# Strassen's seven half-block products for the gate and up projections of a three-block model

## The chip, the cores and the metric

The kernel runs on one core of one Trainium2 chip. The metric is device time in microseconds (us) of one execution; a time of a kernel is the median of its runs. The core has five engines with queues of their own: TensorE (PE; its weight loads are listed as PEld), VectorE (DVE), ScalarE (ACT), GpSimd (POOL) and SyncE (SP, which here issues DMAs). Each works through its queue in order and waits on semaphores for the others.

## The reference

A hidden state x of 512 tokens and 1024 features goes through three blocks: attention with compressed, selected and windowed keys; two layers of sparse and differential attention; and a state-space branch beside a delta rule. Each of the four layers ends in a gated feed-forward of inner width 2816, all in float32:

```
h = rms_norm(x, g)
gate, up = h @ w_gate, h @ w_up            # 1024 -> 2816 each
x = x + (silu(gate) * up) @ w_down         # layers 2, 3 and 4
# layer 1: up passes a causal convolution of width 3 first, then
# a, g = split(up);  x = x + (silu(g) * a) @ w_down
```

## The kernel before

Features lie on the 128 partitions and the 512 tokens along the free dimension, so x is eight tiles of 128x512. Every float32 operand of a large product is split in two float32r parts, hi and lo, and a product of a 128x128 weight tile with a 128x512 tile of x is three matmuls (`mm3`, L347 to L352): hi·hi, hi·lo, lo·hi. `load_piece` (L277) fetches a block of weights of 128x1024 by DMA (`wraw`, a ring of 4), ACT casts it to `whi` (L283) and DVE subtracts to get `wlo` (L284); `whi` and `wlo` have rings of 3 (WS). `lin_T` (L295) runs eight k-tiles of three matmuls into one PSUM bank.

A feed-forward (`ffn`, L1617) handles its 22 pairs of a gate block and an up block (128 inner features each) in two halves of 11, each followed by the down projection of that half (`out_proj`, L1628). For three of the four layers a pair is `swiglu` (L1606): product for the gate, DVE multiply by the row of 1/rms (`rbc`, L1610), Silu on ACT (L1611), a second multiply by `rbc` on POOL (L1612), product for up, DVE multiply with it (L1614), and the split of the result into `acth` and `actl` (L291, L292). In the first layer (`ff`, L843) each of the two products is multiplied by `rbc` (L848), convolved by an ACT operation (L851) and two DVE steps (L856), and gated (L858, L859).

`out_proj` of the mixer, ahead of the feed-forward, adds to x (L1634), makes the operand hi and lo of x·g for the feed-forward (`norm_in`, L467 on ACT and L468 on DVE), and adds squares of x into a sum (`stat_add`, L434 on ACT, L436 on POOL).

The order of the instructions of each engine is set by the framework's scheduler when the program is built; no table of the kernel sets it. Tiles of a ring are given out in turn, and a writer waits until the last reader of its slot is done.

Of the kernel before, what the change touches and what calls it, by code (L numbers as in the profile page):

```python
# [197 lines left out]
# ---------------------------------------------------------------- device code  # L198
class Build:
# [141 lines left out]
    def scaled(self, o, scale, name):  # L341
        """o * scale in two parts."""
# [4 lines left out]
    def mm3(self, out, w, x, start=True, stop=True):  # L347
        """out (+)= w.T @ x, either operand in two parts."""
# [5 lines left out]
    def scores(self, q, k, qt, masks, mx, sm):  # L354
        """Per half: exp(max - (q.k + mask)) with its row sums; q carries the turned sign."""
# [19 lines left out]
    def turned(self, t, qt):  # L375
        """[queries, keys] -> the blocks of keys on partitions, [128, block, 128 queries]."""
# [10 lines left out]
    def rsqrt(self, y, v, pool=False):  # L387
        """y = v ** -0.5 on small [128, n] tiles; v is SBUF and positive."""
# [17 lines left out]
    def bcast_cols(self, col_of_tt, tag="at"):  # L406
        """[128 tokens, 128 (broadcast)] stationary per token tile -> PSUM [128, 512] rows."""
# [5 lines left out]
    def bcast_pairs(self, cols, tag="at"):  # L413
        """cols [128 tokens, 4, 2] -> PSUM [128 = (2, 64), 512]."""
# [4 lines left out]
    # sums of squares of the residual stream, and what follows from them  # L419
# [19 lines left out]
    def col_sums(self, *accs):  # L439
        """-> PSUM [128 tokens, 4]: sums over the partitions."""  # L440
# [9 lines left out]
    def stat_end(self, st):  # L450
        """-> [128 tokens, 4]: 1 / rms"""
# [21 lines left out]
    # ------------------------------------------------------------ block 1  # L473
    def block1(self, x, B, first, g_next, stats):
# [36 lines left out]
        # the overlapping windows of the compressed keys and values, position pairs on partitions  # L511
# [99 lines left out]
        # relative bias strips, sign turned: strip[p, h, c] = -bias[bucket(p + 384 - c)], masked where negative  # L611
# [30 lines left out]
        # the two halves of the spatial gating unit, in parts that go between others  # L642
# [28 lines left out]
        # q / k norms per head  # L671
# [16 lines left out]
        # compressed branch probabilities, transposed to [(r, n), q]  # L688
# [85 lines left out]
        # selected and windowed branches, head pair by head pair: scores ahead of transposes and values, with parts  # L774
        # of projections in between
# [59 lines left out]
        hg = self.out_proj(x, self.aps["b1_wout"][:, :, :512], mix, B["g_ffn"], [st])  # L835
# [3 lines left out]
        # convolved gated feed-forward, in two halves of its width  # L839
        wup = self.aps["b1_wup"]  # L840
        self.set_ring(cv=3)

        def ff(f):  # L843
            cv = []
            for h in range(2):
                ps = self.lin_T(wup[2 * f + h], hg)
                up = self.r512("cv")
                nc.vector.tensor_tensor(up, ps, rbc, op=ALU.mult)  # L848
# [31 lines left out]
    def block2(self, l, x, xg, st, G, g_next, stats):  # L880
# [38 lines left out]
        # index scores and the 128 largest per query  # L919
# [54 lines left out]
        # A unit is a pair of heads (two maps of one, or two that share a block of rows), a step a unit's tile of  # L974
        # queries: scores two steps ahead, then transposes, then values, with parts of projections in between.
# [44 lines left out]
        # sparse attention over the selected keys  # L1020
# [725 lines left out]
```

## Time and profile before

| | before |
|---|---|
| median of three runs | 3123.3 us (3119.72 to 3123.72) |
| span of the profiled execution | 3123.8 us (with nothing listed around it) |
| PE busy | 3052.9 us, 98% |
| DVE busy | 1785.8 us, 57% |
| ACT busy | 1231.4 us, 39% |
| POOL busy | 440.5 us, 14% |
| bytes moved by DMA | 299.95 MB, mean 96 GB/s |

Busy time is the time in which an engine has at least one instruction under way. A matmul's record is longer than the distance from its start to the next one's start, since matmuls overlap; the pace of PE is read from starts. An instruction's record on DVE or POOL begins when the engine takes it up and includes any time that it stands before it can move data.

### The profile page before, as it was taken

To read this page: it belongs to the slowest core of one execution; us is meant where nothing else is said; L and a number is where in the kernel's file an instruction comes from. 1 tells how busy PE (TensorE), PEld (TensorE's weight loads), DVE (VectorE), ACT (ScalarE), POOL (GpSimd) and SP (SyncE) were. 2 spreads that over 40 slices of the span, in tenths; PEclk is the share of its full clock that TensorE was granted. 3 is DMA by queue.
4 is the path that set the end of the run, shared out by engine and by line. 5 is a ranking of instruction groups with operands and counts; after the bars stand their busy time and mean duration, and the time that the engine had idled before them with its cause. 6 is when DMAs were issued, how large, how long until landed. Compare 5 with 4: busy or idle time off the path is not lost.

```text
span 3123.8 us, 40875 instructions
## 1 busy us (share of the span) xinstructions
PE 3052.9 (98%) x15416; PEld 2437.1 (78%) x15416; DVE 1785.8 (57%) x3400; ACT 1231.4 (39%) x2261; POOL 440.5 (14%) x411
## 2 busy tenths in 40 slices
PE   8999999999999999999999999999999999999998
PEld 6867888887677888887677888877777888888886
DVE  6576655647976333348866333369874665543333
ACT  4365433434455222234454222347543433322222
POOL 0001000011221101121211101110820000211011
PEclk9999999998999999998899999999999999999999
DMA  5402223332212223332213233236434222322322
GB/s 175 125 22 77 90 80 109 99 100 81 74 52 92 95 81 108 97 99 80 72 47 99 93 91 102 79 107 199 155 99 155 85 86 88 108 95 78 110 83 74
DMA packets 124052, 299.95 MB, mean 96 GB/s; under 512 B 28440, under 2 KB 40792, under 8 KB 123856
## 3 DMA queue, kind: packets, MB, share of 16 engines
q1 hardware_dynamic: 115696, 285.79, 29.2%
q10 hardware_dynamic: 7680, 9.97, 1.2%
q8 instruction: 122, 2.00, 0.3%
q0 software_dynamic: 480, 1.57, 0.1%
q14 instruction: 74, 0.61, 0.1%
HBM read 272.52 MB, written 14.79 MB: 92 GB/s over the span
## 4 chain that ended last, share of the span: by engine, by line
PE 87%; DVE 6%; DMA 2%; ACT 2%; POOL 1%; issue 1%; ACTq 1%; SPq 0%; DVEq 0%; POOLq 0%
PE p L350 24%; PE p L351 24%; PE p L352 24%; PE s L362 2%; DMA rope<-rope 2%; PE tr L382 1%; PE ss L444 1%; PE p L333 1%; ACTq L874 1%; DVE isc L925 1%; PE O L1036 1%; PE p L335 1%; PE p L334 1%; POOL rope L877 1%; DVE m L924 1%
## 5 line engine op out<-in xcount | busy, mean ns | idle before, releaser
L350 PE MATMUL p<-xh,whi 128*128 128x512 f32 x2360 | 955.4, 405 | 10.6 <-ACT xh L467 7.2
L283 ACT CAST whi<-wraw 128x1024 fp32r<-128x1024 f32 (+4 forms) x528 | 495.5, 940 | 1181.3 <-PE p L351 851.5
L351 PE MATMUL p<-xl,whi 128*128 128x512 f32 x2360 | 949.4, 402 | 0.5 <-DVE xl L468 0.5
L352 PE MATMUL p<-xh,wlo 128*128 128x512 f32 x2360 | 946.5, 401 | 1.1 <-DMA wraw<-in_b_cw1k 1.1
L284 DVE TENSOR_TENSOR wlo<-wraw,whi 128x1024 fp32r<-128x1024 f32 (+4 forms) x528 | 599.9, 1138 | 325.1 <-ACT whi L283 311.9
L350 PEld LDWEIGHTS p<-xh,whi 128*128 128x128 f32 x2360 | 448.4, 190 | 120.9 <-issue 8.8
L352 PEld LDWEIGHTS p<-xh,wlo 128*128 128x128 f32 x2360 | 447.5, 190 | 107.5 <-issue 4.8
L351 PEld LDWEIGHTS p<-xl,whi 128*128 128x128 f32 x2360 | 448.2, 190 | 103.1 <-issue 5.0
L350 PE MATMUL p<-acth,whi 128*128 128x512 f32 x704 | 277.8, 395 | 0.0
L352 PE MATMUL p<-acth,wlo 128*128 128x512 f32 x704 | 277.7, 394 | 0.0
L351 PE MATMUL p<-actl,whi 128*128 128x512 f32 x704 | 277.5, 394 | 0.0
L1612 POOL TENSOR_TENSOR g<-g,rbc 128x512 f32<-128x512 f32 x66 | 114.0, 1728 | 808.5 <-ACT g L1611 808.5
L436 POOL TENSOR_TENSOR sqacc<-sqacc,sq 128x512 f32<-128x512 f32 x63 | 97.4, 1550 | 777.0 <-ACT sq L434 776.8
L1614 DVE TENSOR_TENSOR g<-g,p 128x512 f32<-128x512 f32 x66 | 45.4, 688 | 238.7 <-PE p L352 238.7
L352 PEld LDWEIGHTS p<-acth,wlo 128*128 128x128 f32 x704 | 132.2, 188 | 31.6
L351 PEld LDWEIGHTS p<-actl,whi 128*128 128x128 f32 x704 | 132.2, 188 | 31.5
L350 PEld LDWEIGHTS p<-acth,whi 128*128 128x128 f32 x704 | 132.2, 188 | 31.3
L1610 DVE TENSOR_TENSOR g<-p,rbc 128x512 f32<-128x512 f32 x66 | 45.7, 692 | 188.1 <-PE p L352 188.1
L369 ACT ACTIVATE stile<-stile,sm 128x128 f32<-128x128 f32 (+3 forms) x192 | 106.8, 557 | 83.3 <-DVE sm L366 72.1
L1634 DVE TENSOR_TENSOR x<-x,p 128x512 f32<-128x512 f32 x96 | 66.0, 688 | 108.1 <-PE p L352 107.9
L333 PE MATMUL p<-whi,xh 128*128 128x256 f32 (+2 forms) x352 | 104.6, 298 | 0.3 <-ACT rope L871 0.3
L334 PE MATMUL p<-wlo,xh 128*128 128x256 f32 (+2 forms) x352 | 102.9, 293 | 0.0
(457 smaller groups left out, 4183.4 us busy)
## 6 DMA issues: line engine op xcount, KB each, us to landing
wraw<-in_b_wup SPq DMA_DIRECT2D x176, 512.0 KB, 3.3
wraw<-in_b_win SPq DMA_DIRECT2D x118, 512.0 KB, 3.6
wraw<-in_b_wdn SPq DMA_DIRECT2D x64, 512.0 KB, 3.5
wraw<-in_b_wout SPq DMA_DIRECT2D x48, 256.0 KB, 2.7
wraw<-in_b_wdn SPq DMA_DIRECT2D x64, 192.0 KB, 2.3
rope<-rope ACTq DMA_DIRECT2D x128, 64.0 KB, 2.3
row<-rows SPq DMA_DIRECT2D x32, 256.0 KB, 4.4
wraw<-in_b_wtC SPq DMA_DIRECT2D x8, 512.0 KB, 4.0
```

Of the source, the lines that this page charges most:

```text
L283: nc.scalar.copy(hi, raw)
L284: nc.vector.tensor_tensor(lo, raw, hi.bitcast(F32), op=ALU.subtract)
L333: mm(ps, xs[k][0][:, ts], wh[:, s], start=k == 0, stop=False)
L334: mm(ps, xs[k][0][:, ts], wl[:, s], start=False, stop=False)
L350: mm(out, w[0], x[0], start=start, stop=False)
L351: mm(out, w[0], x[1], start=False, stop=False)
L352: mm(out, w[1], x[0], start=False, stop=stop)
L362: self.nc.tensor.matmul(out[g][:, :n], q[i][hs, qt * P : n], k[j][hs, :n], start=c == 0, stop=c == 2)
L369: nc.scalar.activation(t[:, :n], t[:, :n], AF.Exp, bias=mx[:, g : g + 1], scale=-1.0, accum_out=sm[:, g : g + 1])
L436: eng.tensor_tensor(accs[i], accs[i], sq, op=ALU.add)
L1612: nc.gpsimd.tensor_tensor(g, g, rbc, op=ALU.mult)
L1634: nc.vector.tensor_tensor(x[m], x[m], ps, op=ALU.add)
```

## The change

The products of a pair, the weight blocks A (gate above up, 256 inner features) by h (1024 features by 512 tokens), are taken as a 2x2 block product: A is halved by output (gate, up) and by features (k-tiles 0 to 3, 4 to 7), h by features and by tokens (0 to 255, 256 to 511). Strassen's algorithm, in Winograd's form, makes it from seven products of half blocks in place of eight: 84 matmuls of 256 columns for a pair in place of 48 of 512. The seven need sums of blocks on both sides.

- On the side of h, `Forms` makes them once per feed-forward, in the `out_proj` of the mixer, in place of `norm_in`.
- On the side of the weights, `load_pair` makes four sums of 128x512 per pair on POOL, and splits seven blocks of 128x512 in hi and lo (one split of 1024 columns and five of 512).
- `pair_steps` runs the products (PSUM banks 0 to 5) and combines them: two copies on ACT, five adds with a PSUM input on DVE, two adds on POOL, each of 256 columns. The up half comes out with its sign turned, and the last multiply turns it back.

New rings of four slots each: `ws` (sums of weights), `wa` (the seventh block in two parts), `gu` (gate and up).

```diff
+    def load_pair(self, wa, wb):
+        ...
+        a11, a12, a21, a22 = (r[:, o : o + T] for r in raws for o in (0, T))
+        s1, s2, s4, s3 = (self.r512("ws") for _ in range(4))
+        for o, i, j in ((s1, a21, a22), (s2, s1, a11), (s4, s2, a12), (s3, a11, a21)):
+            nc.gpsimd.tensor_tensor(o, i, j, op=ALU.add)
+        ...
+        both = self.split(raws[0], tiles=parts())
+        f = {"a11": [t[:, :T] for t in both], "a12": [t[:, T:] for t in both]}
+        for names, srcs in ((("s1", "s2"), (s1, s2)), (("s4", "s3"), (s4, s3)), (("a22",), (a22,))):
+            tiles = parts() if len(names) == 2 else [self.r512("wa", F32R) for _ in range(2)]
+            for i, (name, src) in enumerate(zip(names, srcs)):
+                f[name] = self.split(src, tiles=[t[:, i * T : (i + 1) * T] for t in tiles])
+        return f
+
+    def pair_steps(self, wa, wb, xf, g, u):
+        ...
+        def product(w, x):
+            ps = self.pst("st", "st")[:, :H]
+            for k in range(KT // 2):
+                c = slice(k * P, (k + 1) * P)
+                self.mm3(ps, [t[:, c] for t in f[w]], xf.parts[x][k], k == 0, k == KT // 2 - 1)
+            return ps
+
+        add = nc.vector.tensor_tensor
+        nc.scalar.copy(g[:, lo], product("a11", "b11"))
+        nc.scalar.copy(u[:, hi], product("s1", "t5"))
+        add(u[:, lo], g[:, lo], product("s2", "t6"), op=ALU.add)
+        add(g[:, lo], g[:, lo], product("a12", "b21"), op=ALU.add)
+        add(g[:, hi], u[:, hi], product("s4", "b22"), op=ALU.add)
+        nc.gpsimd.tensor_tensor(g[:, hi], g[:, hi], u[:, lo], op=ALU.add)
+        add(u[:, lo], u[:, lo], product("s3", "t7"), op=ALU.add)
+        nc.gpsimd.tensor_tensor(u[:, hi], u[:, hi], u[:, lo], op=ALU.add)
+        add(u[:, lo], u[:, lo], product("a22", "t4"), op=ALU.add)
...
     def swiglu(self, w, f, hg, rbc):
-        pg = self.lin_T(w[2 * f], hg)
-        g = self.tmp(name="g")
-        nc.vector.tensor_tensor(g, pg, rbc, op=ALU.mult)
+        g, u = self.r512("gu"), self.r512("gu")
+        last_of(self.pair_steps(w[2 * f], w[2 * f + 1], hg, g, u))
+        nc.vector.tensor_tensor(g, g, rbc, op=ALU.mult)
         nc.scalar.activation(g, g, AF.Silu)
         nc.gpsimd.tensor_tensor(g, g, rbc, op=ALU.mult)
-        pu = self.lin_T(w[2 * f + 1], hg)
-        nc.vector.tensor_tensor(g, g, pu, op=ALU.mult)
+        nc.vector.scalar_tensor_tensor(g, g, -1.0, u, op0=ALU.mult, op1=ALU.mult)
         return self.split(g, "act")
...
+class Forms:
+    def keep(self, src, *where):
+        both = self.b.split(src, "xf")
...
+    def add(self, m, x, g):
+        ...
+        if m < 4:
+            u = self.u[k] = b.t512(name="xu")
+            nc.scalar.activation(u, x, AF.Copy, scale=g)
+            nc.vector.tensor_tensor(u[:, hi], u[:, lo], u[:, hi], op=ALU.subtract)
+            self.keep(u, ("b11", k), ("t5", k))
+            return
+        ...
+        nc.scalar.activation(w, x, AF.Copy, scale=g)
+        nc.vector.scalar_tensor_tensor(t6, w[:, hi], -1.0, u[:, hi], op0=ALU.mult, op1=ALU.subtract)
+        self.keep(w, ("b21", k), ("b22", k))
+        nc.vector.scalar_tensor_tensor(v[:, hi], t6, -1.0, w[:, lo], op0=ALU.mult, op1=ALU.subtract)
+        nc.vector.scalar_tensor_tensor(v[:, lo], t6, -1.0, u[:, lo], op0=ALU.mult, op1=ALU.subtract)
+        if k % 2:
+            self.keep(self.t6, ("t6", k - 1), ("t6", k))
+        self.keep(v, ("t7", k), ("t4", k))
```

In the convolved feed-forward of the first layer the two products are replaced in the same way; the gate's half is then multiplied by `rbc` on POOL (L909 of the changed kernel) and the up half on DVE (L907).

Two places in the order show what stands in the queues. The first is DVE, in the middle of the first half of the first swiglu feed-forward, before the change: two pairs.

```order
L1610 TENSOR_TENSOR g_9849<-p_9824,rbc_9390 128x512
L284 TENSOR_TENSOR wlo_9927<-wraw_9924,whi_9926 128x1024
L1614 TENSOR_TENSOR g_9849<-g_9849,p_9859 128x512
L284 TENSOR_TENSOR wlo_9963<-wraw_9960,whi_9962 128x1024
L292 TENSOR_TENSOR actl_9886<-g_9849,acth_9885 128x512
L1610 TENSOR_TENSOR g_9920<-p_9895,rbc_9390 128x512
L284 TENSOR_TENSOR wlo_9998<-wraw_9995,whi_9997 128x1024
L1614 TENSOR_TENSOR g_9920<-g_9920,p_9930 128x512
L284 TENSOR_TENSOR wlo_10034<-wraw_10031,whi_10033 128x1024
L292 TENSOR_TENSOR actl_9957<-g_9920,acth_9956 128x512
```

At the same place after the change one pair (gu_11624, gu_11625) has fourteen rows, of which these are the first twelve (L1676, the product with the up half, and L292 for `actl` follow); `st` are the PSUM tiles of the products, `ws` the sums of weights, and the `wlo` rows make the parts of the next pair, the `wa` row those of the pair after it.

```order
L514 TENSOR_TENSOR gu_11625<-gu_11624,st_11686 128x256
L292 TENSOR_TENSOR wlo_11781<-wraw_11768,whi_11780 128x1024
L516 TENSOR_TENSOR gu_11624<-gu_11624,st_11700 128x256
L292 TENSOR_TENSOR wlo_11785<-ws_11772,whi_11784 128x512
L518 TENSOR_TENSOR gu_11624<-gu_11625,st_11714 128x256
L292 TENSOR_TENSOR wlo_11785<-ws_11773,whi_11784 128x512
L1673 TENSOR_TENSOR gu_11624<-gu_11624,rbc_11054 128x512
L521 TENSOR_TENSOR gu_11625<-gu_11625,st_11729 128x256
L292 TENSOR_TENSOR wlo_11791<-ws_11774,whi_11790 128x512
L292 TENSOR_TENSOR wlo_11791<-ws_11775,whi_11790 128x512
L524 TENSOR_TENSOR gu_11625<-gu_11625,st_11744 128x256
L292 TENSOR_TENSOR wa_11939<-wraw_11912,wa_11938 128x512
```

Five rows a pair have become fourteen, and the splits of weights, which stood one per product, stand between the adds of the pair in work.

The second place is POOL, at the same point of the program, before the change: five pairs.

```order
L1612 TENSOR_TENSOR g_9423<-g_9423,rbc_9390 128x512
L1612 TENSOR_TENSOR g_9494<-g_9494,rbc_9390 128x512
L1612 TENSOR_TENSOR g_9565<-g_9565,rbc_9390 128x512
L1612 TENSOR_TENSOR g_9636<-g_9636,rbc_9390 128x512
L1612 TENSOR_TENSOR g_9707<-g_9707,rbc_9390 128x512
```

After the change, one pair (gu_11624, gu_11625); the `ws` rows are the sums of weights of the pair after next.

```order
L482 TENSOR_TENSOR ws_11914<-wraw_11912 128x512
L519 TENSOR_TENSOR gu_11624<-gu_11624,gu_11625 128x256
L482 TENSOR_TENSOR ws_11915<-ws_11914,wraw_11910 128x512
L522 TENSOR_TENSOR gu_11625<-gu_11625 128x256
L482 TENSOR_TENSOR ws_11916<-ws_11915,wraw_11910 128x512
L1675 TENSOR_TENSOR gu_11624<-gu_11624,rbc_11054 128x512
L482 TENSOR_TENSOR ws_11917<-wraw_11910,wraw_11912 128x512
```

One row a pair has become seven, and the pair's own two sums and its multiply stand between the sums for a later pair.

## Rows read from the trace of the kernel before

**Rows 1.** The page's first part: busy us (share of span) xinstructions.
```profile
PE 3052.9 (98%) x15416; PEld 2437.1 (78%) x15416; DVE 1785.8 (57%) x3400; ACT 1231.4 (39%) x2261; POOL 440.5 (14%) x411
```
**Rows 2.** Windows, a swiglu half: us, then PE, PEld, DVE, ACT, POOL busy, PEclk.
```profile
1194.00:1305.00 111.00, 111.00 (x479) 89.73 (x478) 43.88 (x50) 31.24 (x40) 17.98 (x10) 1.00 0.28 89
```
**Rows 3.** Timeline of POOL, same half: start us, duration us, engine, line, operation.
```profile
1228.11 1.80 POOL L1612 TENSOR_TENSOR g<-g,rbc 128x512 f32<-128x512 f32 x1 [9.36 <-ACT g L1611]
1239.27 1.80 POOL L1612 TENSOR_TENSOR g<-g,rbc 128x512 f32<-128x512 f32 x1 [9.36 <-ACT g L1611]
```
**Rows 4.** Timeline of PE, same half: matmuls of 512 columns.
```profile
1232.02 0.39 PE L350 MATMUL p<-xh,whi 128*128 128x512 f32 x1
...
1232.71 0.39 PE L350 MATMUL p<-xh,whi 128*128 128x512 f32 x1
```
**Rows 5.** Timeline of PE, first layer's projections: matmuls of 256 columns.
```profile
135.78 0.41 PE L335 MATMUL p<-whi,xl 128*128 128x256 f32 x1
135.99 0.42 PE L333 MATMUL p<-whi,xh 128*128 128x256 f32 x1
...
136.37 0.28 PE L335 MATMUL p<-whi,xl 128*128 128x256 f32 x1
...
136.72 0.28 PE L335 MATMUL p<-whi,xl 128*128 128x256 f32 x1
```
**Rows 6.** Timeline of POOL in the last block, operations back to back.
```profile
2059.35 1.29 POOL L436 TENSOR_TENSOR sqacc<-sqacc,sq 128x512 f32<-128x512 f32 x1 [4.62 <-ACT sq L434]
2060.59 0.52 POOL L1288 MEMSET sys<- 128x512 f32 x1
...
2230.72 0.65 POOL L1298 TENSOR_TENSOR subst<-sys,sys 128x255 f32<-128x255 f32 x1
```
**Rows 7.** Timeline of DVE, a split of 1024 columns and its successor.
```profile
994.88 1.23 DVE L284 TENSOR_TENSOR wlo<-wraw,whi 128x1024 fp32r<-128x1024 f32 x1 [0.21 <-ACT whi L283]
996.02 0.75 DVE L468 SCALAR_TENSOR_TENSOR xl<-x,pack,xh 128x512 fp32r<-128x512 f32 x1
```
**Rows 8.** Timeline of DVE and POOL, the first layer's out projection.
```profile
292.34 1.34 POOL L436 TENSOR_TENSOR sqacc<-sqacc,sq 128x512 f32<-128x512 f32 x1 [140.26 <-ACT sq L434]
293.09 0.69 DVE L1634 TENSOR_TENSOR x<-x,p 128x512 f32<-128x512 f32 x1 [0.56 <-PE p L352]
293.69 0.69 DVE L284 TENSOR_TENSOR wlo<-wraw,whi 128x512 fp32r<-128x512 f32 x1
```
**Rows 9.** Lines by form: count | busy us, mean ns of one | idle before.
```profile
L292 DVE TENSOR_TENSOR actl<-g,acth 128x512 fp32r<-128x512 f32 x66 | 45.2, 685 | 0.0
...
L366 DVE CUSTOM_DVE_ANT_0 stile<-s,b_cmask 128x256 f32<-128x256 f32 x16 | 6.6, 414 | 0.9 <-PE s L362 0.9
...
L856 DVE SCALAR_TENSOR_TENSOR cv<-cv,pack,cv 128x511 f32<-128x511 f32 x44 | 32.8, 746 | 0.8 <-ACT cv L851 0.8
...
L291 ACT CAST acth<-g 128x512 fp32r<-128x512 f32 x66 | 41.0, 622 | 0.0
```
**Rows 10.** Timeline of DVE and POOL where both work, in the second block.
```profile
1489.02 0.69 DVE L876 TENSOR_TENSOR rope<-rope,tab 128x512 f32<-128x512 f32 x1
1489.15 1.70 POOL L875 TENSOR_TENSOR rope<-rope,tab 128x512 f32<-128x512 f32 x1 [7.42 <-DMA rope<-rope]
1489.63 2.30 DVE L284 TENSOR_TENSOR wlo<-wraw,whi 128x1024 fp32r<-128x1024 f32 x1
1490.93 2.12 POOL L877 TENSOR_TENSOR rope<-rope,rope 128x512 f32<-128x512 f32 x1
```
**Rows 11.** Windows, the out projection ahead of the second feed-forward.
```profile
984.50:1003.50 19.00, 18.26 (x83) 14.67 (x82) 15.43 (x19) 12.61 (x19) 7.99 (x6) 1.00 0.53 167
```
**Rows 12.** Windows, a stretch with pauses between matmuls (index scores).
```profile
741.00:748.30 7.30, 6.64 (x26) 4.54 (x28) 6.53 (x13) 3.78 (x8) 0.14 (x1) 0.50 0.00 0
```

More of the change, by code (lines that the diff above doesn't have):

```diff
@@ L834, in block1 @@
         st = self.stat()
-        hg = self.out_proj(x, self.aps["b1_wout"][:, :, :512], mix, B["g_ffn"], [st])
+        hg = Forms(self)
+        self.out_proj(x, self.aps["b1_wout"][:, :, :512], mix, B["g_ffn"], [st], forms=hg)
         self.free(mix)
@@ L840, in block1 @@
         wup = self.aps["b1_wup"]
-        self.set_ring(cv=3)
+        self.banks(mm=(6, 7), at=(7,), st=range(6))
         def ff(f):
             cv = []
[L845 to L848, printed above, removed]
+            ups = self.r512("gu"), self.r512("gu")
+            last_of(self.pair_steps(wup[2 * f], wup[2 * f + 1], hg, *ups))
+            for h, up in enumerate(ups):
+                if h:
+                    nc.vector.scalar_tensor_tensor(up, up, -1.0, rbc, op0=ALU.mult, op1=ALU.mult)
+                else:
+                    nc.gpsimd.tensor_tensor(up, up, rbc, op=ALU.mult)
                 cw = lambda j: B["conv_w"][:, f * 6 + h * 3 + j : f * 6 + h * 3 + j + 1]
@@ L860, in ff @@
             return self.split(cv[0], "act")
-        r = self.ffn(x, ff, self.aps["b1_wdn"], hg, rbc, g_next, stats)
-        self.set_ring(cv=0)
-        return r
+        return self.ffn(x, ff, self.aps["b1_wdn"], hg, rbc, g_next, stats)
     def rope(self, ps, dim, cs, sn):
@@ L1122, in block2 @@
         st2 = self.stat()
-        hg = self.out_proj(x, A["wout"][:, :, :512], mix, G[f"g_ffn{l}"], [st2])
+        hg = Forms(self)
+        self.out_proj(x, A["wout"][:, :, :512], mix, G[f"g_ffn{l}"], [st2], forms=hg)
         self.free(mix)
         rbc2 = self.bcast_row(self.stat_end(st2))
+        self.banks(mm=(6, 7), at=(7,), st=range(6))
         return self.ffn(x, lambda f: self.swiglu(A["wup"], f, hg, rbc2), A["wdn"], hg, rbc2, g_next, stats)
@@ L1598, in block3 @@
         st2 = self.stat()
-        hg = self.out_proj(x, self.aps["b3_wout"], mg, Q["g_ffn"], [st2])
+        hg = Forms(self)
+        self.out_proj(x, self.aps["b3_wout"], mg, Q["g_ffn"], [st2], forms=hg)
         self.free(mg)
         rbc2 = self.bcast_row(self.stat_end(st2))
+        self.banks(mm=(6, 7), at=(7,), st=range(6))
         return self.ffn(
@@ L1622, in ffn @@
         act = [ff(f) for f in range(h, FF)]
-        self.free(hg, rbc)
+        self.free(hg.tiles, rbc)
+        self.set_ring(ws=0, wa=0, gu=0)
         r = self.out_proj(x, wdn[:, :, h * P :], act, g_next, stats)
@@ L1626, in ffn, with out_proj @@
         return r
-    def out_proj(self, x, w, xs, g, stats, ms=range(KT)):
+    def out_proj(self, x, w, xs, g, stats, ms=range(KT), forms=None):
         nc = self.nc
@@ L1634, in out_proj @@
             nc.vector.tensor_tensor(x[m], x[m], ps, op=ALU.add)
-            if g is not None:
+            if forms is not None:
+                forms.add(m, x[m], g[:, m : m + 1])
+            elif g is not None:
                 t = (self.t512(F32R, "xh"), self.t512(F32R, "xl"))
@@ L1650, in gelu2, with __init__ @@
         return out
+class Forms:
+    def __init__(self, b):
+        self.b, self.tiles, self.u = b, [], {}
+        self.parts = {n: [None] * 4 for n in ("b11", "b21", "b22", "t4", "t5", "t6", "t7")}
+    def keep(self, src, *where):
+        both = self.b.split(src, "xf")
+        self.tiles += both
+        for i, (name, k) in enumerate(where):
+            self.parts[name][k] = [t[:, i * T // 2 : (i + 1) * T // 2] for t in both]
+    def add(self, m, x, g):
+        b, nc, k = self.b, self.b.nc, m % 4
+        lo, hi = slice(0, T // 2), slice(T // 2, T)
+        if m < 4:
[4 more added lines that the diff above has]
+            return
+        u, w, v = self.u[k], b.tmp(name="xw"), b.tmp(name="xv")
+        if k % 2 == 0:
+            self.t6 = b.tmp(name="xt6")
+        t6 = self.t6[:, (lo, hi)[k % 2]]
+        nc.scalar.activation(w, x, AF.Copy, scale=g)
[6 more added lines that the diff above has]
+        self.keep(v, ("t7", k), ("t4", k))
+        b.free(u)
 def last_of(steps):
```

19 lines of the change are left out of this document (added).

## Prediction

> **What bounds the kernel now.** I read the page's busy table first: TensorE (PE) is busy 3052.9 us of a 3123.8 us span, 98% [rows 1]. Then the windows over half of a feed-forward: in 111 us PE has no idle time, at clock 1.00, VectorE (DVE) is busy for 43.9 us and GpSimd (POOL) for 18.0 us [rows 2]. POOL's one instruction per pair of gate and up blocks repeats every 11.16 us [rows 3]; PE's 512-column matmuls start 0.69 us apart for three, 0.23 each [rows 4], and 48 of them make 11.1. So a pair is now pure PE time, 88 pairs are 982 us, and everything else hides below. The question is whether the work that Strassen adds still hides.
>
> The profiled span of 3123.8 is 0.5 us above the median of the runs (3123.3), so the sum goes by the span and needs no correction.
>
> **What PE gives back.** A pair takes 7 products of 4 k-tiles of 3 matmuls, 84 with 256 columns. Where 256-column matmuls ran at full clock, three starts took 0.35 us, 0.117 each [rows 5], so 84 are 9.83 us: 1.33 us saved per pair, 117 us in all. That is the whole possible gain.
>
> **What DVE and POOL get.** Per pair of the 66 swiglu pairs, POOL had one 512-column multiply; it now has four sums of weight blocks (L482), that multiply, and two 256-column sums (L519, L522). A POOL tensor_tensor of 512 columns is 1.29 us, 1.24 from start to start; one of 255 columns 0.65 [rows 6]. That is 5 x 1.24 + 2 x 0.65 = 7.5 us. DVE now has one 1024-column split, five 512-column splits of weight blocks, the rbc multiply, the last product and the split of the result, and five 256-column adds from PSUM. A 1024 split costs 1.14 from start to start [rows 7], a 512-column operation 0.69, or 0.61 behind another [rows 8, 9], a 256-column one from PSUM 0.41, or 0.34 behind another [rows 9]. So 1.14 + 8 x 0.61 = 6.0 us with both inputs in SBUF, plus 5 x 0.34 = 1.7 from PSUM: 7.7 us. Each engine alone would fit under 9.83. ScalarE (ACT), whose 512-column cast is 0.62 [rows 9], and the DMAs, of the same weights and bytes, stay under it too.
>
> **Together they don't fit.** A DVE operation with two SBUF inputs and a POOL operation do not run at once in this trace [rows 10]. A DVE split that takes 1.23 us elsewhere [rows 7] was issued at 1489.63 while POOL worked, and took 2.30; the POOL multiply behind it was issued at 1490.93 and took 2.12 in place of 1.29, since it waited for that split; and the POOL one before it took 1.70, having found DVE at work. Each waits out the whole of the other's instruction, and the waiter goes next. An add whose one input is in PSUM isn't held up: it took 0.69 beside a working POOL [rows 8]. The Trainium skill states this as a rule (SBUF — State Buffer, section "SBUF: two separate sides"): the port pair that DVE and GpSimd share is an exclusive lock, held for a whole instruction. By that rule, the trace agrees. Before, only 1.8 us of POOL per pair met it, with DVE 60% idle.
>
> So a swiglu pair needs the shared access for 7.5 + 6.0 = 13.5 us, which is a lower bound of its period, and 13.5 + 1.7 = 15.2 plus handoffs if nothing overlaps. Walking the order of the changed program (in the section on the change) decides between. POOL's sum for the pair after next may start only once DVE's fourth row has read the old sum out of the ring of four; its L519 waits for the g add, and DVE's rbc multiply, queued right behind, waits for L519; DVE's subtraction-and-product L1676 waits for POOL's multiply, which waits for Silu; then DVE stands 0.76 us for ACT's cast (0.62 and two handoffs of 0.07), and POOL has nothing left to do until the next pair's fourth DVE row. Not covered are thus that 0.76, about 0.85 of the PSUM adds ahead of the fourth and behind it, another add of 0.35 between the rbc multiply and its successor, and about 0.4 of waiting for an ACT cast: 2.3. I take 13.5 + 2.3 = **15.8 us** per pair against 11.16. PE, which needs 9.83, then waits 6 us per pair.
>
> **The 22 pairs of the convolved feed-forward.** POOL: four sums, one multiply, two half sums, 7.5 us, where it had nothing. DVE with two SBUF inputs: 1.14 + 5 x 0.61 for weights, four convolution steps and one rbc multiply at 0.67 (0.75 in the rows less the 0.08 of a queue) [rows 9], the product and a split at 0.61: 8.8 us. The sum is 16.3, with the PSUM adds 18.0; a strict walk, in which the weight parts stand behind the last product's add, gives 19.8. I take **17.8 us**.
>
> **Building the operand forms** (Forms.add, in the projection ahead of each feed-forward). Before, DVE was busy 15.4 of 19 us there [rows 11]. Now DVE has 14 splits of 512, 16 operations of 256 columns, eight adds of x from PSUM, the last weight splits and the first pair's parts, about 22.5 us with two SBUF inputs (25 x 0.61 + 16 x 0.38 + 1.14), and POOL 6 sums of squares and 8 weight sums, 14 x 1.24 = 17.4: 40 us of shared access in a section that took some 24. PE's first products need only early forms, so not all of it is exposed: 0 to 20 us each, I take 13.
>
> **The sum.** A half of a feed-forward has 11 pairs, and its last makes no parts for a successor, so 10 periods and one of about 11 us, against 122.8. Swiglu: 158 + 11 - 122.8 = +46.2, six halves +277. Convolved: 178 + 11 - 122.8 = +66.2, two halves +132. Forms: 4 x 13 = +52. The down projections keep their matmuls and stay bound by PE. 3123.8 + 461 = **3585 us**.
>
> Bounds: with shared access alone (13.5, 16.3, forms at 0) the halves give 6 x 22 + 2 x 50 = +232, 3356. With nothing overlapping (16.5, 19.8, forms 20 each) 6 x 53 + 2 x 86 + 80 = +570, 3694.
>
> **Rivals.**
> 1. *Faster: PE stays the bound.* If parts made two pairs ahead keep PE fed, each pair takes 9.83, and the time is 3123.8 - 117 + 0 to 30 for the forms, about 3020. The point that decides is whether DVE and POOL together stay under 9.83 us per pair, which needs them to run at once. Each alone does (7.7 and 7.5); against it stand the stretched rows [rows 10]. 5%.
> 2. *The queues run ahead and only shared access counts*: about 3356 to 3430. For it: POOL works up to two pairs ahead. Against it: rings of four blocks, so POOL stops each cycle until DVE has read. 14%.
> 3. *TensorE's clock falls.* PE would pause some 6 us in 16. In a stretch with pauses before each product the granted clock was 0.50, the 1.2 GHz level [rows 12], and 256-column matmuls then start 0.21 apart [rows 5]: 84 are 17.6 us, above the swiglu period. With 18.5 and 19.5 per period, and 15 for the last pair, the halves give 6 x 77 + 2 x 87 = +636, with forms about 3810. Against it: here PE still streams over 60% of the time. The Trainium skill (TensorE: Matmul & The Clock Gate, section "HAM oscillation") warns of such pauses between bursts. 10%.
> 4. *Nothing is shared and only the order's waits count*: 7.7 of DVE, 0.76 for ACT and some 3 of waiting for L519 and the multiply are 11.4 per swiglu pair, by the same count 13.5 per convolved one, 6 x 1 + 2 x 22 + 30 more than before, near 3200. The rows against rival 1 are against this too. 3%.
>
> **How the numbers follow.** The forecast, by its own range 3440 to 3700, has 68%; the rivals 14, 10, 5 and 3. Runs of this kernel spread over 4 us, so 0.2% (6 us) is about what can be told from no change. Only rival 1 is faster: 5%. A result within 0.2% needs lost cover to cancel 117 us by chance: 2%. Slower: 93%. The range for 8 in 10 is 3400 to 3720: it leaves out the fast rivals, the clock rival, and the low end of rival 2.
>
> **What would show it.** Right: POOL busy more than twice its 440 us with rows of L482 far above 1.29; DVE splits of 512 above 0.69, many near 1.9; PE with long idle before products, released by DVE; swiglu pairs 15 to 17 us apart. Wrong: PE near 98% busy (rival 1); pairs at 13.5 (rival 2); clock well under 1 in the feed-forwards (rival 3); L482 at 1.29 throughout, so that the rows of before do not carry over.

## The result, and the profile after

The changed kernel took **3465.5 us** (median of four runs, 3455.9 to 3473.7) against 3121.5 us for the kernel before on the same chip: a ratio of 1.109, 95% interval 1.106 to 1.112. It is 344 us slower; the forecast was 3585, with a range of 3400 to 3720. The profiled execution has a span of 3454.1 us, 330.3 more than the one of before, and the accounts below go by that.

First the busy table of the page (engine, us, share of span, instructions), against [rows 1].

```profile
PE 3121.6 (90%) x18584; PEld 2645.6 (77%) x18584; DVE 2496.8 (72%) x4258; ACT 1458.8 (42%) x2845; POOL 1190.1 (34%) x961
```

POOL is busy 2.7 times as long as before, DVE 711 us longer. PE's 69 us more stand beside less work: its matmuls ran at half clock for part of the time (below). No engine is at 98% any more: 90% is the most, and the chain of waits changes hands (shares of the span by engine; before, PE had 87% and DVE 6%):

```profile
PE 44%; DVE 15%; POOL 7%; issue 7%; ACT 4%; DMA 2%; ACTq 1%; SPq 0%; DVEq 0%; POOLq 0%
```

The window over a steady stretch of a swiglu half (us, then PE, PEld, DVE, ACT and POOL busy, granted clock, DMA share, GB/s) answers to [rows 2]: PE now has 19 us without work in 110, and TensorE's clock is 0.84 in place of 1.00.

```profile
1370.00:1480.00 110.00, 90.95 (x626) 87.87 (x625) 90.05 (x102) 37.43 (x71) 70.46 (x53) 0.84 0.21 65
```

The copy of a pair's first product (L510, ACT) marks the period, in the timeline of the same half (start, duration), against the 11.16 of [rows 3]:

```profile
1343.16 0.37 ACT L510 COPY gu<-st 128x256 f32<-128x256 f32 x1 [0.46 <-PE st L352]
1354.69 0.36 ACT L510 COPY gu<-st 128x256 f32<-128x256 f32 x1
1369.80 0.36 ACT L510 COPY gu<-st 128x256 f32<-128x256 f32 x1
...
1475.63 0.36 ACT L510 COPY gu<-st 128x256 f32<-128x256 f32 x1
1488.18 0.36 ACT L510 COPY gu<-st 128x256 f32<-128x256 f32 x1
```

The first interval of the half is 11.5 us, the next eight 15.1 each, the last 12.5. One whole period, in the timelines of DVE and POOL put together by start, shows why (compare [rows 6, 8, 10]; x2 in a row is two operations in a row, with one duration for both):

```profile
1409.07 0.69 DVE L292 TENSOR_TENSOR wlo<-ws,whi 128x512 fp32r<-128x512 f32 x1
1409.67 0.42 DVE L518 TENSOR_TENSOR gu<-gu,st 128x256 f32<-128x256 f32 x1
1409.84 1.30 POOL L482 TENSOR_TENSOR ws<-wraw 128x512 f32<-128x512 f32 x1 [4.69 <-DVE wlo L292]
1410.01 1.68 DVE L292 TENSOR_TENSOR wlo<-ws,whi 128x512 fp32r<-128x512 f32 x1
1411.10 1.19 POOL L519 TENSOR_TENSOR gu<-gu,gu 128x256 f32<-128x256 f32 x1
1412.24 1.29 POOL L482 TENSOR_TENSOR ws<-ws,wraw 128x512 f32<-128x512 f32 x1
1412.32 1.76 DVE L1673 TENSOR_TENSOR gu<-gu,rbc 128x512 f32<-128x512 f32 x1 [0.63 <-POOL gu L519]
1414.00 0.41 DVE L521 TENSOR_TENSOR gu<-gu,st 128x256 f32<-128x256 f32 x1
1414.33 1.83 DVE L292 TENSOR_TENSOR wlo<-ws,whi 128x512 fp32r<-128x512 f32 x2
1414.49 1.11 POOL L522 TENSOR_TENSOR gu<-gu 128x256 f32<-128x256 f32 x1 [0.96 <-DVE gu L521]
1415.57 1.75 POOL L482 TENSOR_TENSOR ws<-ws,wraw 128x512 f32<-128x512 f32 x1
1416.08 0.41 DVE L524 TENSOR_TENSOR gu<-gu,st 128x256 f32<-128x256 f32 x1
1416.41 1.45 DVE L292 TENSOR_TENSOR wa<-wraw,wa 128x512 fp32r<-128x512 f32 x1
1417.27 1.73 POOL L1675 TENSOR_TENSOR gu<-gu,rbc 128x512 f32<-128x512 f32 x1
1418.97 1.29 POOL L482 TENSOR_TENSOR ws<-wraw,wraw 128x512 f32<-128x512 f32 x1
1419.04 1.78 DVE L1676 SCALAR_TENSOR_TENSOR gu<-gu,gu 128x512 f32<-128x512 f32 x1 [1.18 <-POOL gu L1675]
1421.51 0.69 DVE L292 TENSOR_TENSOR actl<-gu,acth 128x512 fp32r<-128x512 f32 x1 [0.68 <-ACT acth L291]
1422.11 0.42 DVE L514 TENSOR_TENSOR gu<-gu,st 128x256 f32<-128x256 f32 x1
1422.72 1.23 DVE L292 TENSOR_TENSOR wlo<-wraw,whi 128x1024 fp32r<-128x1024 f32 x1 [0.19 <-ACT whi L291]
1423.86 0.42 DVE L516 TENSOR_TENSOR gu<-gu,st 128x256 f32<-128x256 f32 x1
1424.19 0.69 DVE L292 TENSOR_TENSOR wlo<-ws,whi 128x512 fp32r<-128x512 f32 x1
```

The split issued at 1409.07 finds POOL idle and takes 0.69; the same split at 1410.01 finds a sum under way and takes 1.68; POOL's L519, begun at 1411.10 behind that split, takes 1.19 where an operation of 255 columns took 0.65 before [rows 6]. The two engines take turns. The add at 1416.08, with one input in PSUM, takes 0.41 beside a working POOL. Averaged, in the lines by form (count | busy us, mean ns of one | idle before), against the 685 and 1290 of [rows 6, 9]:

```profile
L292 DVE TENSOR_TENSOR wlo<-ws,whi 128x512 fp32r<-128x512 f32 x352 | 357.6, 1034 | 8.1 <-ACT whi L291 8.1
L482 POOL TENSOR_TENSOR ws<-ws,wraw 128x512 f32<-128x512 f32 x176 | 271.3, 1542 | 54.4 <-DVE wlo L292 32.5 <-DVE rcol L394 6.5 <-ACT whi L291 6.1
```

And the table of waits (engine, tile and line, what was waited for: us in total, times, longest) names who is late for PE, and why POOL doesn't run ahead:

```profile
POOL ws L482 <- DVE wlo L292: 297.4, 86, 6.4
...
PE st L352 <- DVE wlo L292: 119.6, 121, 3.1
```

### The profile page after: what moved, and what is told of

It is laid out like the page before. It is cut to its first block, busy times and chain, and to the rows that moved or that the text cites. A ratio compares the mean times of both kernels' runs of the same rounds, so it can differ in the third digit from the quotient of the medians.

```text
span 3454.1 us, 49895 instructions
## 1 busy us (share of the span) xinstructions
PE 3121.6 (90%) x18584; PEld 2645.6 (77%) x18584; DVE 2496.8 (72%) x4258; ACT 1458.8 (42%) x2845; POOL 1190.1 (34%) x961
## 4 chain that ended last, share of the span: by engine, by line
PE 44%; DVE 15%; POOL 7%; issue 7%; ACT 4%; DMA 2%; ACTq 1%; SPq 0%; DVEq 0%; POOLq 0%
PE p L350 10%; PE p L351 9%; PE p L352 9%; DVE wlo L292 4%; PE st L352 3%; PE st L350 2%; PE st L351 2%; DVE gu L1676 2%; POOL gu L1675 2%; PE s L362 2%; ACT whi L291 1%; POOL ws L482 1%; DMA rope<-rope 1%; DVE wlo L284 1%; POOL sys L1364 1%
## 5 line engine op out<-in xcount | busy, mean ns | idle before, releaser
L352 PE MATMUL st<-xfh,wlo 128*128 128x256 f32 x2112 | 655.2, 313 | 119.9 <-DVE wlo L292 119.6
L350 PE MATMUL st<-xfh,whi 128*128 128x256 f32 x2112 | 650.8, 309 | 106.7 <-ACT whi L291 101.8
L351 PE MATMUL st<-xfl,whi 128*128 128x256 f32 x2112 | 641.2, 305 | 1.2 <-DVE xfl L292 0.9
L284 DVE TENSOR_TENSOR wlo<-wraw,whi 128x1024 fp32r<-128x1024 f32 (+5 forms) x352 | 388.0, 1104 | 247.7 <-ACT whi L283 244.1
L352 PEld LDWEIGHTS st<-xfh,wlo 128*128 128x128 f32 x2112 | 451.3, 215 | 147.8 <-DVE wlo L292 147.5
L350 PEld LDWEIGHTS st<-xfh,whi 128*128 128x128 f32 x2112 | 454.7, 215 | 122.3 <-ACT whi L291 117.6
L351 PEld LDWEIGHTS st<-xfl,whi 128*128 128x128 f32 x2112 | 453.9, 215 | 2.2 <-DVE xfl L292 2.0
L350 PE MATMUL p<-xh,whi 128*128 128x512 f32 (+1 forms) x952 | 399.6, 420 | 15.3 <-ACT xh L467 7.0
L351 PE MATMUL p<-xl,whi 128*128 128x512 f32 (+1 forms) x952 | 393.3, 413 | 0.0
L352 PE MATMUL p<-xh,wlo 128*128 128x512 f32 (+1 forms) x952 | 390.9, 411 | 1.3 <-DVE wlo L284 1.3
L292 DVE TENSOR_TENSOR wlo<-ws,whi 128x512 fp32r<-128x512 f32 x352 | 357.6, 1034 | 8.1 <-ACT whi L291 8.1
L482 POOL TENSOR_TENSOR ws<-ws,wraw 128x512 f32<-128x512 f32 x176 | 271.3, 1542 | 54.4 <-DVE wlo L292 32.5
L482 POOL TENSOR_TENSOR ws<-wraw 128x512 f32<-128x512 f32 x88 | 126.8, 1440 | 461.8 <-DVE wlo L292 253.8
L351 PEld LDWEIGHTS p<-xl,whi 128*128 128x128 f32 (+1 forms) x952 | 184.2, 194 | 38.6 <-issue 4.3
```

The costliest lines, as they stand in the source:

```text
L284: nc.vector.tensor_tensor(lo, raw, hi.bitcast(F32), op=ALU.subtract)
L292: self.nc.vector.tensor_tensor(lo, src, hi.bitcast(F32), op=ALU.subtract)
L350: mm(out, w[0], x[0], start=start, stop=False)
L351: mm(out, w[0], x[1], start=False, stop=False)
L352: mm(out, w[1], x[0], start=False, stop=stop)
L482: nc.gpsimd.tensor_tensor(o, i, j, op=ALU.add)
```

## The experiments

The theory (A in the expectations): DVE operations with two SBUF inputs and POOL operations exclude each other, and what both need per pair is the period. Its main rival (B): nothing is shared, and the queues' order and waits make the period.

**Everything on DVE.** The seven POOL operations of a pair move, `nc.gpsimd.tensor_tensor` becoming `nc.vector.tensor_tensor`:

```diff
-            nc.gpsimd.tensor_tensor(o, i, j, op=ALU.add)
+            nc.vector.tensor_tensor(o, i, j, op=ALU.add)
...
-        nc.gpsimd.tensor_tensor(g[:, hi], g[:, hi], u[:, lo], op=ALU.add)
+        nc.vector.tensor_tensor(g[:, hi], g[:, hi], u[:, lo], op=ALU.add)
...
```

> The seven POOL operations of a pair (four sums of weights, two half sums, one multiply) are issued on DVE instead; everything else as in the changed kernel. Theory A (DVE operations with two SBUF inputs and POOL operations exclude each other): a swiglu pair's shared access falls from 7.5 of POOL and 6.0 of DVE to DVE alone, 6.0 + 1.7 + 5 x 0.61 + 2 x 0.33 = 11.4 us, with the wait for ACT's cast about 12.2 against the 15.1 measured; a convolved pair about 15 against 16.4; 60 x -2.9 + 20 x -1.4 = -202, about 3260 us, and no DVE split above 0.75. Theory B (DVE's own queue and its waits for other engines set the period, nothing is shared): 3.7 us more in that queue, less about 1.5 of waits for POOL, gives 17 us a pair, about 3630 us.

Measured: 3256.2 us (ratio to before 1.044, 1.041 to 1.048), 209 us less than the changed kernel. More work on the engine that is waited for made the kernel faster, which A forecast and B did not. The lines by form of this kernel show every split of 512 at 0.68, and the sums, now at half of POOL's time:

```profile
L292 DVE TENSOR_TENSOR wlo<-ws,whi 128x512 fp32r<-128x512 f32 x352 | 231.0, 682 | 13.5 <-ACT whi L291 13.5
...
L482 DVE TENSOR_TENSOR ws<-ws,wraw 128x512 f32<-128x512 f32 x176 | 120.1, 682 | 0.1
```

DVE is now nearly full, as the window over a swiglu half has it (103.57 of 106 us); its periods alternate between 9 or 10 us and 13 to 15, 11.3 to 12.2 on average by half.

```profile
1300.00:1406.00 106.00, 97.78 (x775) 95.55 (x774) 103.57 (x193) 54.20 (x92) 0.00 (x0) 0.95 0.27 85
```

**Sums made and not read; sums not made.** Two kernels that differ from each other only in whether POOL does the four sums. The first:

```diff
         s1, s2, s4, s3 = (self.r512("ws") for _ in range(4))
         for o, i, j in ((s1, a21, a22), (s2, s1, a11), (s4, s2, a12), (s3, a11, a21)):
             nc.gpsimd.tensor_tensor(o, i, j, op=ALU.add)
+        s1, s2, s4, s3 = a21, a22, a12, a11
```

The second:

```diff
-        s1, s2, s4, s3 = (self.r512("ws") for _ in range(4))
-        for o, i, j in ((s1, a21, a22), (s2, s1, a11), (s4, s2, a12), (s3, a11, a21)):
-            nc.gpsimd.tensor_tensor(o, i, j, op=ALU.add)
+        s1, s2, s4, s3 = a21, a22, a12, a11
```

> POOL still makes the four sums of weights of each pair, but nothing reads them: the splits take the raw weight blocks in their place (so the weight sums are left out of the result). The amount of work on every engine is unchanged; the waits of ACT's casts and DVE's splits for the sums are gone, and the sums' ring no longer waits for DVE. Theory A (shared access): the 13.5 us of a swiglu pair remain, so its period stays at 13.5 to 15.1, total 3350 to 3455 us, and L482 stays near 1.5 us. Theory B (waits set by the order): the period falls to 11 to 12 us, total 3110 to 3200 us.

> The four sums of weights per pair are left out altogether; the splits take the raw blocks (so the result lacks the sums). Theory A (shared access): 8.5 us of shared access remain in a swiglu pair (2.5 of POOL, 6.0 of DVE), with the 1.7 of PSUM adds and 0.8 for ACT's cast about 11.0 against 15.1, a convolved pair about 13 against 16.4: 60 x -4.1 + 20 x -3.4 = -314, about 3140 us; far below the kernel whose sums are made and not read. Theory B (waits set by the order): the same as that kernel within 1%, since POOL had idle time to make the sums.

Measured: 3437.6 us (1.102, 1.099 to 1.104) and 3116.5 us (0.998, 0.996 to 0.9996). Without any wait for the sums, the steady swiglu period fell only from 15.1 to 14.0; without the sums it fell to 10.7. So 1.1 us of the 15.1 belongs to the waits for the sums, and 321 us of the total to sums that nobody reads, made by POOL beside DVE. (That is by the swiglu pairs; in the first layer, by the adds to x, the unread sums cost 14 us more than the read ones.) The windows over a swiglu half of the two:

```profile
1370.00:1480.00 110.00, 92.57 (x660) 85.98 (x659) 89.21 (x111) 42.60 (x80) 79.82 (x55) 0.93 0.22 72
```
```profile
1250.00:1320.00 70.00, 67.92 (x570) 67.11 (x569) 60.04 (x92) 34.83 (x66) 25.74 (x20) 1.00 0.30 98
```

PE is at 84% of the first and 97% of the second. How the sums cost 3.3 us a period is in rows of the two kernels, at the same place of a pair. First with the sums:

```profile
1409.64 1.43 DVE L292 TENSOR_TENSOR wlo<-wraw,whi 128x512 fp32r<-128x512 f32 x1
1412.19 0.74 POOL L520 TENSOR_TENSOR gu<-gu,gu 128x256 f32<-128x256 f32 x1
1412.96 0.69 DVE L1674 TENSOR_TENSOR gu<-gu,rbc 128x512 f32<-128x512 f32 x1 [1.89 <-POOL gu L520]
```

Then without them:

```profile
1268.66 0.68 DVE L292 TENSOR_TENSOR wlo<-wraw,whi 128x512 fp32r<-128x512 f32 x1
1269.97 0.69 DVE L1671 TENSOR_TENSOR gu<-gu,rbc 128x512 f32<-128x512 f32 x1 [0.63 <-POOL gu L517]
```

Three splits of a pair are 2.1 us longer in all beside the sums (1.81 for 1.23, 1.45 and 1.43 for 0.68 each), with their inputs ready: that is the shared access itself. The other 1.3 is DVE's wait for POOL's half sum, 1.89 in place of 0.63, because the half sum stands behind the weight sums in POOL's queue. These sums are themselves stretched by turns, but a share of that wait is POOL's queue and not the access; the two kernels don't part them. The estimate of 11.0 for the kernel without sums was 0.3 too long.

**The products alone.** One set of parts per half (`self.fixed` is emptied ahead of each):

```diff
-        f = self.load_pair(wa, wb)
+        f = self.fixed = self.fixed or self.load_pair(wa, wb)
```

> The weight blocks of only the first pair of each half are loaded, summed and split, and all eleven pairs use them (the other pairs' weights are left out of the result). What is left per pair is PE's 84 matmuls and the combination of the products. Theory A: with the weight work gone nothing holds PE, a pair takes 9.83 us at granted clock 1.00, against 11.16 before the change, so 3124 - 88 x 1.33 = 3007, plus 10 to 40 for building the forms: 3010 to 3050 us. Rival: the products themselves are slower than reckoned (PE pauses between them and its clock falls, or the combination is a chain of its own): a pair above 11 us, more than 3124 us.

Measured: 3079.9 us (0.987, 0.983 to 0.990), 30 above the expectation's upper end. Swiglu pairs took 9.8 to 9.9 us, as 84 x 0.117 says, with PE never idle at clock 1.00 (window of such a half):

```profile
1230.00:1310.00 80.00, 80.00 (x684) 80.00 (x683) 33.43 (x65) 14.65 (x33) 21.92 (x25) 1.00 0.00 1
```

The convolved pairs took 11.06, not 9.83: 22 x 1.2 = 27 us, which is about the miss. There something in a pair other than the weights holds it up; what it is stays open. So in the swiglu pairs the price of the products was right, and Strassen's gain is there when nothing else is late; in the convolved pairs, at 11.06 against 11.16 before, nearly all of the gain is missing even then.

**The operand forms.** All forms read from the plain splits of x·g:

```diff
-            nc.vector.tensor_tensor(u[:, hi], u[:, lo], u[:, hi], op=ALU.subtract)
...
-        nc.vector.scalar_tensor_tensor(t6, w[:, hi], -1.0, u[:, hi], op0=ALU.mult, op1=ALU.subtract)
         self.keep(w, ("b21", k), ("b22", k))
-        nc.vector.scalar_tensor_tensor(v[:, hi], t6, -1.0, w[:, lo], op0=ALU.mult, op1=ALU.subtract)
-        nc.vector.scalar_tensor_tensor(v[:, lo], t6, -1.0, u[:, lo], op0=ALU.mult, op1=ALU.subtract)
-        if k % 2:
-            self.keep(self.t6, ("t6", k - 1), ("t6", k))
-        self.keep(v, ("t7", k), ("t4", k))
+        for n in ("t6", "t7", "t4"):
+            self.parts[n][k] = self.parts["b21"][k]
```

> The sums and differences of the operand of x are left out: the forms t4, t5, t6 and t7 are read from the plain splits (so the result is made from other operands), and six splits and sixteen 256-column operations go from each of the four out projections, about 9.7 us of DVE and 4 of ACT. Theory A (the forms are exposed, 10 to 14 us a feed-forward by the difference between first and second halves): 20 to 45 us less than the changed kernel, 3420 to 3445 us. Theory B (the forms are hidden, the first half's extra is the start of its pairs): within 8 us of 3465.

Measured: 3440.1 us (1.101, 1.099 to 1.103), 25 less than the changed kernel: A, at its lower part. By the adds to x the first halves of the four feed-forwards gave back 7.5, 3.0, 4.6 and 10.6 us, the second halves about nothing.

**TensorE's clock.** In the changed kernel the granted clock swings within each pair. Windows of 1.7 us, from a steady stretch:

```profile
1406.80:1408.50 1.70, 0.51 (x2) 0.30 (x2) 1.51 (x3) 1.70 (x3) 0.00 (x0) 1.00 0.63 229
1408.50:1410.20 1.70, 1.32 (x6) 1.32 (x7) 1.70 (x5) 1.15 (x3) 0.36 (x1) 0.63 0.30 43
1410.20:1411.90 1.70, 1.70 (x10) 1.70 (x10) 1.49 (x1) 0.00 (x0) 1.70 (x2) 0.50 0.73 265
...
1413.60:1415.30 1.70, 1.70 (x17) 1.70 (x16) 1.70 (x4) 1.19 (x3) 0.81 (x1) 1.00 0.00 0
```

PE waits at the end of a pair, works at the 1.2 GHz level (0.50: 10 matmuls a window instead of 17) soon after it resumes, and is back at full clock some us later. Does that cost time? Matmuls into a spare PSUM bank fill PE's waits:

```diff
+            for _ in range(3):
+                nc.tensor.matmul(idle, f["a11"][0][:, :P], xf.parts["b11"][0][0], start=True, stop=True)
             ps = self.pst("st", "st")[:, :H]
```

> Three more 256-column matmuls stand ahead of each product of the changed kernel, 21 a pair, into a PSUM bank that nothing reads; they take 21 x 0.117 = 2.5 us of PE at full clock, in time in which PE mostly waits. Their purpose is to keep TensorE's granted clock up, which was 0.86 in the steady stretches of the changed kernel. Theory A (DVE and POOL set the swiglu period of 15.1 us, and the clock costs nothing): the period and the total stay within 1%, 3440 to 3500 us, whatever the clock does. Theory B (products at half clock are on the path): with a clock above 0.95 the 28% of a period that is granted at half speed would run in half the time, up to 2.1 us less a pair, and the total falls to 3290 to 3400 us.

Measured: 3503.4 us (1.121, 1.118 to 1.125), 1.1% above the changed kernel and just over A's upper end; the clock in the steady window rose from 0.84 to 0.97:

```profile
1380.00:1480.00 100.00, 91.64 (x734) 89.65 (x733) 85.79 (x94) 36.63 (x68) 64.67 (x47) 0.97 0.22 75
```

The steady swiglu period went from 15.1 to 14.8, 2% less where A allowed 1%. The total rose all the same: by the adds to x the first layer took 19 us more, its pairs being 17.0 apart with the 21 extra matmuls, and each swiglu half 2 to 4 us more, its last interval going from 12.5 to 14.3. The fall that B reckoned is not there.

**Sums by DMA.** If shared access is the price, sums made by neither engine should be free. An accumulating DMA adds what it moves to its destination. First for two of the four sums, everything else of POOL on DVE:

```diff
+        for o, i, j in ((s1, wb[:, :T], wb[:, T:]), (s3, wa[:, :T], wb[:, :T])):
+            nc.sync.dma_start(o, i)
+            nc.gpsimd.dma_start(o, j, accum_op=ALU.add)
+        for o, i, j in ((s2, s1, a11), (s4, s2, a12)):
+            nc.vector.tensor_tensor(o, i, j, op=ALU.add)
```

> No POOL arithmetic in a pair: two of the four sums of weights (s1, s3) are made by DMA, a plain load of one block and an accumulating DMA (issued by POOL) of the other; s2 and s4, the half sums and the multiply are on DVE. Theory (shared access, now DVE's alone): DVE has 11.4 - 1.2 = 10.2 us a swiglu pair, with the wait for ACT's cast 11.0 against 11.7 with everything on DVE, a convolved pair about 13.5 against 14.6: 60 x -0.7 + 20 x -1.1 = -64 from 3256, about 3190 us; DMA moves 2 MB a pair, 190 GB/s, which slices of the page have reached (198). Rival (an accumulating DMA is late or slow, and the sums are waited for): above 3256 us, with ACT's casts of the sums waiting for DMA.

Measured: **3115.3 us**, 0.997 of before (0.996 to 0.999), 75 less than expected: the swiglu pairs of the second halves take 9.9 to 10.0 us, not 11.0, with PE and DVE both full (window):

```profile
1240.00:1320.00 80.00, 80.00 (x684) 80.00 (x683) 79.86 (x152) 47.60 (x82) 13.80 (x16) 1.00 0.80 205
```

The 0.8 for ACT's cast, which I added, isn't there: DVE is never idle (79.86 of 80 us), so that wait was covered, presumably by work for other pairs, and its 10.2 were 9.9. All four sums by DMA went the other way:

> All four sums of weights are made by DMA (four plain loads and seven accumulating DMAs of 256 KB a pair); the half sums and the multiply are on DVE. Theory A: DVE has 9.0 us a swiglu pair, with the wait for ACT 9.8, and PE (9.85) sets the period: 60 x -1.8 + 20 x -2.4 from 3256, about 3100 us, under the kernel before. Rival B: DMA moves 3.8 MB a pair, which at the 198 GB/s that slices of the page have reached is 19 us, so the period is 19 us and the total 3700 to 3850 us.

Measured: 4054.6 us (1.298, 1.296 to 1.301); a pair takes 21.5 to 22.4 us on average by half. B, and B's 19 was too little. The waits show it, and the page's queue table of this kernel (packets, MB, share of 16 engines' span) why:

```profile
ACT whi L291 <- DMA ws<-in_b_wup: 858.3, 130, 12.7
```
```profile
q1 hardware_dynamic: 166384, 378.09, 30.3%
q0 software_dynamic: 89184, 163.09, 24.7%
```

The accumulating queue (q0) takes 24.7% of 4061.7 us for 163.1 MB, 6.15 us of all 16 engines per MB; the plain one (q1) 3.26. An accumulated byte costs 1.9 times a plain one (packets of the same 2 KB take 178 ns and 84 ns there, medians), so a pair's 2.1 MB of loads and 1.84 MB of accumulation are 6.8 + 11.3 = 18 us with every DMA engine at work, and at the busy share seen in a half (0.81) 22. Why the share stops at 0.81 isn't shown: POOL's issues also waited 1041 us for earlier landings on the same sum (POOL ws L485 <- DMA in the table of waits), so the order has a part in the 22. In the kernel with two sums the same prices give 8.3 us a pair, still under 9.9.

The last kernel keeps those two sums by DMA in the three swiglu feed-forwards, and has the first layer's feed-forward as before the change:

```diff
-        hg = Forms(self)
-        self.out_proj(x, self.aps["b1_wout"][:, :, :512], mix, B["g_ffn"], [st], forms=hg)
+        hg = self.out_proj(x, self.aps["b1_wout"][:, :, :512], mix, B["g_ffn"], [st])
         ...
+            for h in range(2):
+                ps = self.lin_T(wup[2 * f + h], hg)
```

> The kernel with s1 and s3 by DMA, but the first layer's convolved feed-forward as it was before the change (eight products, the plain operand); the three swiglu feed-forwards keep the seven products. Theory (each feed-forward is set by what bounds it alone): the first layer returns to its time before, 44.1 us less than with the seven products by the adds to x (30.9 + 16.9 - 3.7), the swiglu pairs stay at 9.9: 3115 - 44 = 3071 us, 1.6% under the kernel before. Rival (the gain of the swiglu layers belongs to that run's other differences, or the accumulating DMAs of layer 1 hide something): 3100 us or more.

Measured: **3064.0 us**, 0.981 of before (0.980 to 0.983), faster than both kernels. By the adds to x the first layer is at its time before, and each swiglu feed-forward 18 to 21 us under it (4 to 6 in the first half, with the forms, 14 to 15 in the second).

## Why the prediction was right, and where its sizes were off

**What was asked first: does the added work still hide? It doesn't.** PE fell to 90%, and its waits are for the splits L292, as forecast. The saving of 1.33 us a pair was real in the swiglu pairs (9.83 forecast, 9.8 to 9.9 where only products were left); in the 22 convolved pairs, at 11.06 there, it did not show, so some 27 of the 117 us of possible gain were missing even without the work on the weights. Rival 1 needed DVE and POOL to run at once; the turns in the timeline and 3437.6 against 3116.5 rule that out here.

**That DVE and POOL exclude each other.** The rows of before [rows 8, 10] carried over: beside a sum the split took 1.68, and the add from PSUM 0.41. The Trainium skill (SBUF — State Buffer, section "SBUF: two separate sides") has the rule, for a DVE operation with two SBUF inputs against a POOL operation that reads SBUF. By that rule, the trace agrees. Of the signs named, POOL's busy time (2.7 times), the pairs 15.1 apart and PE's waits for DVE came out; the stretched splits took 1.45 and 1.68 in the rows, not near 1.9; "L482 far above 1.29" only in part: a sum that gets the access at once takes 1.29, one that waits 1.75, and the mean is 1.54.

**The period: 15.1 for 15.8, and 16.4 for 17.8.** This is the first mis-sized term, the 13.5 + 2.3. Both parts can be read end to end in the period shown above, from 1409.07 to 1424.19: the access is in use for 13.3 us of it and free for 1.8. So the 13.5 was nearly right, but by two errors that cancel. An operation that has waited for the access costs less than one started behind its own kind: the split of 1410.01 ends at 11.69, L519 then at 12.29, L482 at 13.53, L1673 at 14.08; from end to end, a DVE operation of 512 takes 0.55 where I reckoned 0.61, and the multiply of 1417.27 ends 1.14 after the split ahead of it, where I reckoned 1.24. One that finds the access free costs more: 0.69 for 0.61, 1.30 for 1.24, 1.23 for 1.14. What was too large is the 2.3 of free time: the wait for the cast of `acth` is 0.69 where I reckoned 0.76, the one for a cast of `whi` 0.19 for 0.4, and the adds L514, L516 and L521, with a handoff, leave about 0.9 where I reckoned 1.2 for the PSUM adds. For the convolved pairs only the interval is read, typically 16.3 to 16.6 in the first half and 15.6 on average in the second.

**The ends of a half.** The second mis-sized term, and the larger. I took ten full periods and a last pair of 11 us. The interval between the first two pairs is 11.5: both had their sums made from 1328.8 to 1347.3, largely during the down projection. The last interval, from 1475.63 to 1488.18, is 12.5: the last weight sum starts 3.8 us into it, and none stands beside the rest, as the timeline of POOL shows at the end of that half:

```profile
1479.46 1.30 POOL L482 TENSOR_TENSOR ws<-wraw,wraw 128x512 f32<-128x512 f32 x1
1485.77 1.11 POOL L519 TENSOR_TENSOR gu<-gu,gu 128x256 f32<-128x256 f32 x1 [5.02 <-DVE gu L518]
```

That is 4.3 + 3.3 off ten periods of 15.8; the eight others at 15.1 are 5.6 off; together 13.2 of the 14.7 by which a swiglu half was over-reckoned.

**The sum** goes by the first adds to x of each projection. For one swiglu half they are, before the change (184.2 us apart):

```profile
1133.77 0.69 DVE L1634 TENSOR_TENSOR x<-x,p 128x512 f32<-128x512 f32 x1 [1.19 <-PE p L352]
...
1318.02 0.69 DVE L1634 TENSOR_TENSOR x<-x,p 128x512 f32<-128x512 f32 x1 [1.17 <-PE p L352]
```

and after it (215.6 apart):

```profile
1288.02 0.69 DVE L1698 TENSOR_TENSOR x<-x,p 128x512 f32<-128x512 f32 x1 [0.35 <-PE p L352]
...
1503.64 0.69 DVE L1698 TENSOR_TENSOR x<-x,p 128x512 f32<-128x512 f32 x1 [0.36 <-PE p L352]
```

All halves read so, in us over before:

| term | forecast | measured |
|---|---|---|
| six swiglu halves | +277 (46.2 each) | +189 (31.5) |
| two convolved halves | +132 (66.2) | +90 (45.2) |
| forms, with the start of the pairs | +52 (13 each) | +59 (21.3, 13.8, 14.0, 10.2) |
| down projections and the rest | 0 | -8 |
| all | +461 | +330 |

The halves are measured in the second half of each feed-forward, the forms as what the first half has over it. The forms' size came out, but not for a reason that was shown, so there was luck in it: the sums and differences, with six of the splits, are only 25 of the 59 by their experiment. The irregular first periods of a first half (16.6, 16.0, 17.6) belong to those 25, since without them these are 15.5, 14.9 and 15.1. Where the other 34 come from no run separates.

**The rivals.** Rival 2 (shared access alone, 13.5 and 16.3) named 3356 to 3430 (the 3356 takes 9.8 us for the last pair; with the forecast's 11 it is 3365); the result lies above that, and its swiglu period of 15.1 is nearer the forecast's 15.8 than the 13.5 of shared access alone. Rival 3 had its first half: the clock fell in each pair, to 0.84 to 0.87 on average in the steady stretches. The Trainium skill (TensorE: Matmul & The Clock Gate, section "HAM oscillation") warns of such pauses between bursts. The second half of the rival, that PE then sets the period, failed: PE still had 19 us without work in 110, and with the clock at 0.97 a period was 0.3 shorter. Part of a gain may have been taken by the extra matmuls themselves; that stays open. Rival 4 (about 3200) is out with the unread sums. The forecast's own step "against it: PE still streams over 60% of the time" was no reason: PE was busy for 91 of 110 us and the clock fell all the same.

## What to carry to other kernels

Before giving work to an idle GpSimd, add up what it and VectorE need of the access they share, per unit of work: the two busy shares may each be small and their sum the bound. Where they clashed here, the work was cheaper on VectorE, which did it in half the time (0.68 against 1.29); operations with a PSUM input did not count. What remains is worth moving to an engine of neither kind (here two sums of four by DMA), up to the point where that one fills: four were far too many.

## What was not expected of the hardware

- An accumulating DMA took 6.15 us of all 16 DMA engines per MB (6.06 in the kernel with two sums: 9.3% of 3107.3 us for 47.7 MB), a plain load 3.26.
- With both kinds in flight DMA moved 205 GB/s at a busy share of 0.80, and PE and DVE were at 100% beside it, so these transfers and DVE's full stream did not hinder each other visibly.
- TensorE's clock fell from 1.00 to 0.50 after PE's wait and rose again, all within a period of 15.1 us.
- A turn at the shared access costs 0.06 to 0.1 us less than a start behind the same engine's own operation.
